# Hybrid mixer and expert block on one core: weight loads of one tile (1 MB) become loads of two (2 MB)

## The chip, the cores and the metric

One core of a Trainium2 chip runs the program; the seven others are idle. The metric is device time in microseconds (us). Before the change it was 1384.95 us, the median of three runs (1383.54 to 1385.8).

## What is computed

All weights are float32 and the batch is 256 tokens of width 2048. Cut to its stages, the reference is:

```
h = x + token_mixer(rmsnorm(x))          # one layer
    proj = h @ w_in                      # 2048 x 6672: q k v g | z | xs bc | dt
    retention(q, k, v) * silu(g)         # 4 heads of 256, two chunks of 128 tokens
    ssd(conv(xs, b, c), dt) * silu(z)    # 16 heads of 64, two chunks of 128 tokens
    concat(both) @ w_out                 # 2048 x 2048
h = h + hier_moe(rmsnorm(h))             # 32 experts in 4 groups; each token goes to 2
    a, u = ht @ w_gate[e], ht @ w_up[e]  # 2048 x 512 each
    out += (silu(a) * u * comb) @ w_down[e]   # 512 x 2048
out = rmsnorm(h)
```

The weights of all 32 experts are read, 384 tiles of 1 MB; those of w_in are 52 tiles and those of w_out 16.

## The kernel before, in words

A weight tile is 128 partitions by 2048 floats: 8 KB a partition, 1 MB, one DMA on SP's queue. The host (`lay_out`) stores each so that a partition's 8 KB stand together.

The program has three stages. **The mixer** takes w_in in 13 chunks of 512 columns, four tiles each (`win_tiles`, `first_tiles` for the first chunk). `load` puts a tile into the pool `ring`, which holds four, and `split` makes of each 128x512 part a rounded copy `wh` (ACT, L285) and a remainder `wl` (DVE, L150) in six stage buffers; TensorE (PE) multiplies both (`form_a` L367 to L369, `form_b` L355 to L357). Convolution, scan, retention and gates are generators that `pump` advances between the products; the tokens' inverse norm is one of them (`rms1`: psr, L264; rm on DVE; rcol on POOL; dg on DVE; psb, L271; rbc). **The output projection** (`out_rows`) does the same with w_out.

**The experts** come in eight groups of four, `NG = 8`. A group takes 16 gate tiles, 16 up tiles and 16 down tiles (`project` and `finish`, matmuls at L950); `gather` brings the tokens' rows, at most 32 an expert, into `xg`, and `back` adds the results (psc, L981). In the last four down tiles of a group each holds 128 output columns, so each is followed by its own `back`. The tiles go into 22 buffers, in an order written out by hand as a string of pool names: pools a (4), b (6), e (6), n (1), o (2) and three of four 8 KB "quarters" (c, d, f), which held the mixer's inputs; the fourth quarter is `xg`:

```
    cycle = "aaaaeeeeeecdfbbbbbb"
    turns = "eeeeeenbbbbb" + "baaaaeeeeeencdfbbbbb" + "o" * ONCE
```

A buffer is loaded again once the matmuls that read it are done. n and o are given up after the first group's up product, so 19 buffers go round. Every DMA signals one of eight semaphores in turn, and SP waits before it issues one for the DMA eight issues ago. A scheduler places the instructions of each engine; the program's text gives the order of the loads.

Of the kernel before, what the change touches and what calls it, by code (L numbers as in the profile page):

```python
# [18 lines left out]
P = 128  # L19
D = 2048  # L20
# [75 lines left out]
def lay_out(inp):  # L96
# [8 lines left out]
    win = np.empty((len(CHUNKS), 4, P, 4, 512), np.float32)  # L105
# [6 lines left out]
    o["wout"] = c(np.stack([wo[ET_ORDER[n], :, n].reshape(4, 4, P, 512).transpose(0, 2, 1, 3) for n in range(4)]))  # L112
    wr = np.concatenate([a["w_router_group"][0], a["w_router_expert"][0]], axis=1)
    o["wr"] = c(wr.reshape(KT, P, 36).transpose(1, 0, 2))
    for n, k in (("gate", "w_expert_gate"), ("up", "w_expert_up")):
        o[n] = c(a[k][0].reshape(NG, GE, KT, P, F).transpose(0, 2, 3, 1, 4))
    wd = a["w_expert_down"][0].reshape(NG, GE, 4, P, 4, 512)
    dn = np.empty((NG, 4, 4, P, GE, 512), np.float32)
    dn[:, :3] = wd[..., :3, :].transpose(0, 4, 2, 3, 1, 5)
    dn[:, 3] = wd[..., 3, :].reshape(NG, GE, 4, P, 4, 128).transpose(0, 4, 3, 1, 2, 5).reshape(NG, 4, P, GE, 512)  # L120
    o["down"] = dn
# [21 lines left out]
def block_kernel(tc, I, out):  # L143
# [36 lines left out]
    qp = sb("quarters")  # L180
# [15 lines left out]
    def quarter(i, n, dt=F32):  # L196
        return qp.tile([P, n, 2048 // n], dt, tag=f"q{i}", name=f"quarter{i}")
# [15 lines left out]
    # the tensor engine's clock rises while the first loads are under way  # L213
# [6 lines left out]
    # ---- normalised input (transposed, its norm weight applied), split into two float32r parts  # L220
    xraw = hp.tile([P, KT, T], F32, tag="h", name="xraw")
    xhs = [quarter(0, 8, F32R), xq.tile([P, 8, T], F32R, name="xh2")]
    xls = [quarter(1, 8, F32R), xq.tile([P, 8, T], F32R, name="xl2")]
# [23 lines left out]
    def squares():  # L247
        # summed over the tiles on the engine that is free
        a, b = quarter(2, 8)[:, :4], quarter(3, 8)[:, :4]
# [50 lines left out]
    def pump(n):  # L300
        # a step of the work that waits: what frees the accumulators first, then the mixers
# [17 lines left out]
    def first_tiles():  # L319
        sp.dma_start(par, I["par"])  # L320
        w = ring.tile([P, 4, 512], F32, tag="w", name="w")
        for a, b in ((0, 1), (1, 2), (2, 4)):
            load_x(a, b)
            sp.dma_start(w[:, a:b], I["win"][0, 0, :, a:b])
        for a, b in ((0, 1), (1, 2), (2, 4)):
            prep_x(a, b)
            for j, wh, wl in split(w[:, a:b], min(SPLIT, b - a)):
                yield a + j, wh, wl
        for i in range(1, 4):
            w = ring.tile([P, 4, 512], F32, tag="w", name="w")  # L330
            for a in (0, 2):
                load_x(4 * i + a, 4 * i + a + 2)
                sp.dma_start(w[:, a:a + 2], I["win"][0, i, :, a:a + 2])
            if i == 3:
                sp.dma_start(con, I["con"])
            for a in (0, 2):
                prep_x(4 * i + a, 4 * i + a + 2)
                for j, wh, wl in split(w[:, a:a + 2], SPLIT):
                    yield 4 * i + a + j, wh, wl

    def win_tiles(ci):
# [3 lines left out]
        for i in range(4):  # L345
            for j, wh, wl in split(load(I["win"][ci, i]), SPLIT):
                yield 4 * i + j, wh, wl
# [26 lines left out]
    # ---- state space mixer: convolution  # L374
# [59 lines left out]
    def step_sizes(xdt):  # L434
        # dt: softplus as max(v, 0) + 2 atanh(e / (2 + e)), e = exp(-|v|)
# [19 lines left out]
        # cumulative sums of dt * a: a row per head and chunk, to be spread over the partitions, and columns  # L455
# [18 lines left out]
    # rotary tables  # L474
# [28 lines left out]
    def scan(xdt):  # L503
        # state space mixer: the two chunks
# [43 lines left out]
    # ---- retention  # L548
# [20 lines left out]
    def retention(qT, kT):  # L569
        # scores[s, l] of a chunk's queries with the keys of its own chunk and of the one before  # L570
# [44 lines left out]
    # ---- gates, norms and the transposed mixer output, split in two  # L615
# [37 lines left out]
    for ci, (n, half) in enumerate(CHUNKS):  # L653
# [26 lines left out]
        elif n == "bc":  # L680
            qT, kT = (quarter(i, 8).rearrange("p (h a) t -> p h a t", h=RH) for i in (2, 3))
# [4 lines left out]
        elif n == "z":  # L686
            if half == 0:
                finish_all(later)
                ys = [quarter(i, 8, F32R).rearrange("p (a k) t -> p a k t", a=2) for i in (2, 3)]
            soon.append(group_norm(half))  # L690
            soon.append(to_yt(xs[:, :, 512 * half:512 * half + 512], 8 + 4 * half, ys[half][:, 0], ys[half][:, 1]))
    yrh, yrl = quarter(0, 8, F32R), quarter(1, 8, F32R)
# [3 lines left out]
    # ---- output projection  # L696
    def acc_pair(pool, tag):
        return [pool.tile([P, 512], F32, tag=tag, name="po") for _ in range(NT)]

    def out_rows(ps, n, ld, i0, i1, ahead=0):  # L700
        # the first tokens' products with the last rows may come ahead of the others'
        late = []
        for i in range(i0, i1):
            for j, wh, wl in split(ld(I["wout"][n, i]), SPLIT):
# [22 lines left out]
    # the first columns take the state space mixer's rows first, while the other rows are made  # L727
# [6 lines left out]
    # ---- residual and router logits; from here one ring takes the weights  # L734
# [5 lines left out]
    cycle = "aaaaeeeeeecdfbbbbbb"  # L740
    turns = "eeeeeenbbbbb" + "baaaaeeeeeencdfbbbbb" + "o" * ONCE
    turns += cycle * ((12 + NG * 48 - 32 - len(turns)) // len(cycle))
    turns = itertools.chain(turns, itertools.cycle("aaaaeeeeeebbbbbb"))

    def slot(n, name="wt"):
        if n in "cdf":
            return quarter("cdf".index(n), 4)
        return rings[n].tile([P, 4, 512], F32, tag="w", name=name)

    def wload(src):  # L750
        w = slot(next(turns))
        sp.dma_start(w, src)
        return w

# [12 lines left out]
    def residual(n):  # L767
        # logits as rows of experts, from two tiles of h at a time in two halves of the array
# [15 lines left out]
    def mean_squares():  # L784
        # of all but the last columns
# [12 lines left out]
    def residual_last(t):  # L798
# [8 lines left out]
        # (the squares themselves go where the transposes were, and aren't read)  # L807
# [6 lines left out]
    # ---- routing: first maximum of the groups, first two maxima of the group's experts  # L814
# [3 lines left out]
    # (the groups' logits are padded to eight columns)  # L818
# [10 lines left out]
    # values to be marked, behind others that don't occur: the largest of the groups, the two largest experts  # L829
# [40 lines left out]
    # the other columns: the retention's rows of all, then the state space mixer's rows of each  # L870
# [15 lines left out]
    def choose(t):  # L886
        # positions in the experts' lists, from 1; 0 where the expert isn't chosen
# [22 lines left out]
    rings["o"] = sb("wonce", bufs=ONCE, reuse_waits="tile")  # L910
# [4 lines left out]
    # ---- experts: groups of four, CAP slots each  # L915
# [22 lines left out]
    def gather(pos, cmb):  # L938
# [3 lines left out]
        xg = quarter(3, KT)  # L942
# [198 lines left out]
```

## Time and profile before

| what | value |
|---|---|
| time, median of three runs | 1384.95 us |
| span of the profiled execution | 1382.1 us (the profile gives no other time of this execution) |
| PE busy | 1109.8 us, 80% |
| DVE, ACT, POOL busy | 416.2, 271.4, 25.0 us |
| read from HBM | 481.65 MB, 350 GB/s over the span |
| SP's queue | 70610 packets, 483.80 MB |

The span runs from the first to the last instruction. A packet is what one DMA engine moves in one piece; the 16 DMA engines work beside each other. "Share" of DMA is the packets' time over the time of 16 engines, and it can pass 100% where packets of an engine overlap. Landing is the time from a DMA's issue to its last byte's signal. MB are millions of bytes in totals; a 1 MB tile is 1,048,576 bytes.

### The profile page before, as it was taken

The numbers are of one execution on the slowest core, as the hardware profiler recorded it, in microseconds if no ns is written. First come the engines' busy times: TensorE is split into PE (matmuls) and PEld (weight loads), VectorE is DVE, ScalarE is ACT, GpSimd is POOL, SyncE is SP. The second block draws the span as 40 slices with busy tenths as digits, with TensorE's granted clock in tenths as the row PEclk, the third lists the DMA queues.
The fourth block names the chain that finished last, engine by engine and source line by source line (L and its number), as shares of the span: only waits on it lengthen the run. The fifth ranks groups of instructions, "written<-read, shape, count | busy, mean of one in ns | idle before, by whom it ended". The sixth has DMA issues, their size and how long they took to land.

```text
span 1382.1 us, 17740 instructions
## 1 busy us (share of the span) xinstructions
PE 1109.8 (80%) x7323; PEld 586.3 (42%) x7323; DVE 416.2 (30%) x842; ACT 271.4 (20%) x504; POOL 25.0 (2%) x29
## 2 busy tenths in 40 slices
PE   7999999999999986686668668666866866686764
PEld 4989999888787441032014103201310320140112
DVE  8577968666555130021002002100200210020013
ACT  5465544465444000000000000000000000000002
POOL 5000000000000000000000000000000000000000
PEclk8999999999999998689669768967976886696677
DMA  7545555585876999999999999999999999999994
GB/s 270 210 159 186 198 186 196 204 324 204 337 279 212 386 419 419 420 419 419 420 420 420 419 420 420 419 420 420 420 420 420 419 419 420 420 419 420 420 419 193
DMA packets 70695, 484.98 MB, mean 351 GB/s; under 512 B 8113, under 2 KB 8785, under 8 KB 13137
## 3 DMA queue, kind: packets, MB, share of 16 engines
q1 hardware_dynamic: 70610, 483.80, 86.8%
q8 instruction: 59, 0.97, 0.3%
q14 instruction: 26, 0.21, 0.0%
HBM read 481.65 MB, written 2.11 MB: 350 GB/s over the span
## 4 chain that ended last, share of the span: by engine, by line
DMA 62%; PE 35%; DVE 1%; issue 1%; ACT 0%; SPq 0%; POOL 0%; POOLq 0%; ACTq 0%; DVEq 0%
DMA wt<-down 19%; DMA wt<-up 17%; DMA wt<-gate 16%; DMA quarter<-gate 4%; PE pb L355 4%; PE pb L357 4%; PE pb L356 4%; PE pf L368 3%; PE pf L369 3%; PE pf L367 3%; DMA quarter<-up 3%; PE po L716 2%; PE po L714 2%; PE po L715 2%; DMA quarter<-down 1%; PE pxg L924 1%
## 5 line engine op out<-in xcount | busy, mean ns | idle before, releaser
L950 PE MATMUL pu<-wt,quarter 128*32 128x512 f32 x904 | 171.8, 856 | 80.0 <-DMA wt<-up 80.0
L950 PE MATMUL pg<-wt,quarter 128*32 128x512 f32 x832 | 154.8, 832 | 76.8 <-DMA wt<-gate 76.8
L150 DVE TENSOR_TENSOR wl<-w,wh 128x512 fp32r<-128x512 f32 x224 | 158.9, 720 | 72.0 <-ACT wh L285 71.0
L150 DVE TENSOR_TENSOR sg<-sg,pu 128x512 f32<-128x512 f32 x8 | 5.5, 688 | 553.0 <-PE pu L950 551.8
L285 ACT ACTIVATE wh<-w 128x512 fp32r<-128x512 f32 x224 | 140.1, 631 | 150.5 <-PE pb L356 74.0
L950 PE MATMUL py<-wt,at 128*32 128x128 f32 (+1 forms) x1672 | 120.1, 406 | 13.7 <-DMA wt<-down 12.9
L950 PEld LDWEIGHTS pu<-wt,quarter 128*32 128x32 f32 x904 | 24.2, 127 | 223.8 <-DMA wt<-up 209.7
L950 PEld LDWEIGHTS pg<-wt,quarter 128*32 128x32 f32 x832 | 19.5, 123 | 201.3 <-DMA wt<-gate 195.6
L981 PE MATMUL psc<-y,swt 128*128 128x128 f32 (+1 forms) x224 | 75.0, 459 | 32.8 <-ACT y L978 32.8
L150 DVE TENSOR_TENSOR acc<-acc,psc 128x128 f32<-128x128 f32 (+1 forms) x98 | 43.2, 459 | 164.8 <-PE psc L981 164.6
L950 PEld LDWEIGHTS py<-wt,at 128*32 128x32 f32 x1672 | 45.3, 110 | 79.7 <-issue 39.1
L935 ACT ACTIVATE swt<-psw 128x256 f32<-128x256 f32 x8 | 3.1, 383 | 335.0 <-PE psw L933 335.0
L978 ACT ACTIVATE y<-py 128x128 f32<-128x128 f32 (+1 forms) x56 | 23.2, 414 | 225.9 <-PE py L950 225.8
L924 PEld LDWEIGHTS pxg<-selr,h 128*128 128x128 f32 x512 | 64.3, 208 | 6.5 <-issue 5.9
L924 PE MATMUL pxg<-selr,h 128*128 128x128 f32 x512 | 66.0, 292 | 0.6 <-ACT mask L1012 0.6
L981 PEld LDWEIGHTS psc<-y,swt 128*128 128x128 f32 x224 | 34.0, 194 | 76.1 <-ACT y L978 63.2
L355 PE MATMUL pb<-xh,wh 128*128 128x256 f32 x224 | 64.2, 286 | 0.0
L355 PE MATMUL pb<-quarter,wh 128*128 128x256 f32 x224 | 63.8, 285 | 0.0
L357 PE MATMUL pb<-quarter,wl 128*128 128x256 f32 x224 | 63.7, 284 | 0.0
L967 ACT ACTIVATE sg<-pg 128x512 f32<-128x512 f32 x8 | 4.8, 597 | 299.5 <-PE pg L950 299.5
L356 PE MATMUL pb<-quarter,wh 128*128 128x256 f32 x224 | 63.4, 283 | 0.0
L357 PE MATMUL pb<-xh,wl 128*128 128x256 f32 x224 | 62.8, 280 | 0.0
(259 smaller groups left out, 1466.2 us busy)
## 6 DMA issues: line engine op xcount, KB each, us to landing
wt<-up SPq DMA_DIRECT2D x113, 1024.0 KB, 19.9
wt<-down SPq DMA_DIRECT2D x113, 1024.0 KB, 19.9
wt<-gate SPq DMA_DIRECT2D x104, 1024.0 KB, 19.9
w<-win SPq DMA_DIRECT2D x48, 1024.0 KB, 4.9
quarter<-gate SPq DMA_DIRECT2D x24, 1024.0 KB, 19.9
quarter<-down SPq DMA_DIRECT2D x15, 1024.0 KB, 19.9
quarter<-up SPq DMA_DIRECT2D x15, 1024.0 KB, 19.9
wt<-wout SPq DMA_DIRECT2D x12, 1024.0 KB, 7.8
```

The lines of the kernel that those rows point to most:

```text
L150: dve.tensor_tensor(o, a, b, op=op)
L285: act.activation(wh, w[:, i:i + n], AF.Copy)
L355: pe.matmul(o, wh[:, s], xh(k), start=(k == 0 and c % 2 == 0), stop=False, skip_group_check=True)
L356: pe.matmul(o, wh[:, s], xl(k), start=False, stop=False, skip_group_check=True)
L357: pe.matmul(o, wl[:, s], xh(k), start=False, stop=(k == KT - 1), skip_group_check=True)
L367: pe.matmul(ps[t], lh(k)[:, s], wh, start=(k == 0), stop=False)
L368: pe.matmul(ps[t], lh(k)[:, s], wl, start=False, stop=False)
L369: pe.matmul(ps[t], ll(k)[:, s], wh, start=False, stop=(k == KT - 1))
L714: pe.matmul(ps[t], yh[:, s], wh, start=(k == 0), stop=False)
L924: pe.matmul(px[:, i], h[:, t, (k0 + i) * P:(k0 + i + 1) * P], selr[:, t], start=(i == 0 and x == 0), stop=(x == NT - 1), skip_group_check= ...
L950: pe.matmul(ps[s], lhsT[:, s], w(j), **k)
L981: pe.matmul(px, swt[:, t * P:(t + 1) * P], y, start=True, stop=True)
```

## The change

Weights are laid out and loaded in pairs of tiles, 16 KB a partition, 2 MB a DMA, in the order in which they are used. The rings hold pairs: `ring` (a) two, b three, e three, n one, o one; the four quarters become two "twins" of 16 KB (c and d), and `xg` gets a pool of its own. That is ten pairs that go round and twelve before the first is used again. The 8 KB for `xg` and the rest come from a smaller DMA scratch (`SCRATCH = 256`). The w_out tiles are paired over column chunks, by `OUT_ORDER`. The last two pairs of the last group are still loaded as four 1 MB halves. The final norm's rows lie in c and d.

```
-RING_A = 4
-RINGS = {"a": RING_A, "b": 6, "e": 6, "n": 1}
-ONCE = 2
+RING_A = 2
+RINGS = {"a": RING_A, "b": 3, "e": 3, "n": 1}
+SCRATCH = 256
+OUT_ORDER = [(0, i) for i in range(4)] + [(n, i) for n in range(1, 4) for i in range(2)]
+OUT_ORDER += [(n, i) for i in (2, 3) for n in range(1, 4)]
...
-        win[i] = w[:, s:s + 512].reshape(4, 4, P, 512).transpose(0, 2, 1, 3)
+        win[i] = w[:, s:s + 512].reshape(2, 8, P, 512).transpose(0, 2, 1, 3)
...
+    o["wexp"] = c(ex.reshape(NG, 24, 2, P, GE, 512).transpose(0, 1, 3, 2, 4, 5).reshape(NG, 24, P, 2 * GE, 512))
...
-    def quarter(i, n, dt=F32):
-        return qp.tile([P, n, 2048 // n], dt, tag=f"q{i}", name=f"quarter{i}")
+    def twin(i, n, dt=F32):
+        return qp.tile([P, 2, n, 2048 // n], dt, tag=f"h{i}", name=f"twin{i}")
...
     def load(src):
-        w = ring.tile([P, 4, 512], F32, tag="w", name="w")
+        w = ring.tile([P, 8, 512], F32, tag="w", name="w")
         sp.dma_start(w, src)
...
+        for i, parts in enumerate((((0, 1), (1, 2), (2, 4), (4, 6), (6, 8)), ((0, 2), (2, 4), (4, 6), (6, 8)))):
+            w = ring.tile([P, 8, 512], F32, tag="w", name="w")
...
-    cycle = "aaaaeeeeeecdfbbbbbb"
-    turns = "eeeeeenbbbbb" + "baaaaeeeeeencdfbbbbb" + "o" * ONCE
-    turns += cycle * ((12 + NG * 48 - 32 - len(turns)) // len(cycle))
-    turns = itertools.chain(turns, itertools.cycle("aaaaeeeeeebbbbbb"))
+    cycle = "aaeeecbbbd"
+    turns = "eeebbb" + "naaeeecbbbdo"
+    turns += cycle * ((6 + NG * 24 - 16 - len(turns)) // len(cycle))
+    turns = itertools.chain(turns, itertools.cycle("aaeeebbb"))
...
+    def stream(src, n, single=0):
+        for i in range(n // 2):
+            w = slot(next(turns))
+            s = src(i)
+            for p in ((0, 4), (4, 8)) if i >= n // 2 - single else ((0, 8),):
+                sp.dma_start(w[:, slice(*p)], s[:, slice(*p)])
+            yield w[:, :4]
+            yield w[:, 4:]
...
-        xg = quarter(3, KT)
+        xg = xgp.tile([P, KT, P], F32, name="xg")
...
+    def group(g):
+        return stream(lambda i: I["wexp"][g, i], 48, 2 if g == NG - 1 else 0)
...
-    nc = bacc.Bacc("TRN2", target_bir_lowering=False, num_devices=1)
+    nc = bacc.Bacc("TRN2", target_bir_lowering=False, num_devices=1, dynamic_dma_scratch_size=SCRATCH)
```

The scheduler places some instructions anew. On PE, in the fourth of the second chunk's 128-row parts (pb is that chunk's sum), the first product of the tokens' norm (psr) stood before like this, and psb nine rows on:

```order
L357 MATMUL pb<-quarter_115,wl 128x256
L355 MATMUL pb<-quarter_115,wh 128x256
L356 MATMUL pb<-quarter_117,wh 128x256
L357 MATMUL pb<-quarter_115,wl 128x256
L264 MATMUL psr<-ones,sq 128x1 x2
L355 MATMUL pb<-quarter_115,wh 128x256
L356 MATMUL pb<-quarter_117,wh 128x256
```

Here PE had products of the chunk to do before and after psr. In the changed program psr and psb stand at the end of the first chunk (pf):

```order
L371 MATMUL pf<-wh,xl_120 128x512
L274 MATMUL psr<-ones,sq 128x1 x2
L281 MATMUL psb<-dg,ones 128x256
L357 MATMUL pb<-twin_118,wh 128x256
L358 MATMUL pb<-twin_118,wh 128x256
L357 MATMUL pb<-twin_118,wh 128x256
L358 MATMUL pb<-twin_118,wh 128x256
L359 MATMUL pb<-twin_118,wl 128x256
```

They are now side by side, with none of the chunk's products between them, and four products with wh alone come before the first with wl. DVE's part of the norm (rm, dg, rbc) stood before behind ten splits, of which the last eight are the second chunk's:

```order
L150 TENSOR_TENSOR wl<-w,wh 128x512 x10
L150 TENSOR_TENSOR wdt<-wdt,par 128x256
L159 TENSOR_SCALAR rm_450<-psr 128x2
L157 TENSOR_SCALAR dg<-con,rcol 128x128 x2
L272 COPY rbc<-psb 128x256
L150 TENSOR_TENSOR wl<-w,wh 128x512 x13
```

In the changed program it stands here:

```order
L157 TENSOR_TENSOR wl<-w,wh 128x512 x2
L166 TENSOR_SCALAR rm_449<-psr 128x2
L164 TENSOR_SCALAR dg<-con,rcol 128x128 x2
L282 COPY rbc<-psb 128x256
L157 TENSOR_TENSOR wl<-w,wh 128x512 x8
```

The two splits ahead are the first chunk's last, so all of the second chunk's splits now come behind rbc. The order of the loads on SP is otherwise as before, with one row of a pair for two of a tile.

## Rows read from the trace of the kernel before

**Rows 1.** The page, busy tenths of 40 slices of 34.55 us, the whole span.
```profile
PE   7999999999999986686668668666866866686764
...
DMA  7545555585876999999999999999999999999994
GB/s 270 210 159 186 198 186 196 204 324 204 337 279 212 386 419 419 420 419 419 420 420 420 419 420 420 419 420 420 420 420 420 419 419 420 420 419 420 420 419 193
```
**Rows 2.** The page, the chain that ended last: shares of the span.
```profile
DMA 62%; PE 35%; DVE 1%; issue 1%; ACT 0%; SPq 0%; POOL 0%; POOLq 0%; ACTq 0%; DVEq 0%
```
**Rows 3.** All waits of PE's queue from 50 to 446 us: total, times, longest.
```profile
PE pht L805 <- DVE h L150: 0.5, 1, 0.5
PE psb L271 <- DVE dg L157: 0.5, 1, 0.5
```
**Rows 4.** The chain in order of time, experts: start us, us, what.
```profile
529.16 19.87 DMA wt<-gate
549.10 19.89 DMA wt<-up
...
1352.86 1.11 PE py L950 x8
```
**Rows 5.** DMA queue from 490 to 1350 us: packets, MB, share of 16 engines.
```profile
DMA packets 49513, 360.89 MB, mean 420 GB/s; under 512 B 5495, under 2 KB 5495, under 8 KB 5495
...
q1 hardware_dynamic: 49472, 360.28, 101.0%
```
**Rows 6.** DMA queue from 241 to 244 us, the load of h alone.
```profile
q1 hardware_dynamic: 79, 1.29, 100.5%
```
**Rows 7.** DMA queue from 110.6 to 111.4 us, one 1 MB tile alone.
```profile
q1 hardware_dynamic: 40, 0.33, 97.5%
```
**Rows 8.** SP's issues around the first use of the experts: start, us, operation.
```profile
420.32 24.64 SPq L752 DMA_DIRECT2D wt<-up  x5
450.52 0.33 SPq L752 DMA_DIRECT2D wt<-down  x1
```
**Rows 9.** PE's timeline, first group's gate product: the third and fourth tile.
```profile
452.56 1.92 PE L950 MATMUL pg<-wt,quarter 128*32 128x512 f32 x16
```
**Rows 10.** PE's timeline around the tokens' norm: start, us, operation [idle before].
```profile
42.28 0.28 PE L355 MATMUL pb<-quarter,wh 128*128 128x256 f32 x1
42.40 0.28 PE L356 MATMUL pb<-quarter,wh 128*128 128x256 f32 x1
...
48.04 0.50 PE L264 MATMUL psr<-ones,sq 128*128 128x1 f32 x4
...
50.10 0.70 PE L271 MATMUL psb<-dg,ones 128*128 128x256 f32 x2 [0.51 <-DVE dg L157]
50.45 0.47 PE L357 MATMUL pb<-quarter,wl 128*128 128x256 f32 x1
```
**Rows 11.** DVE's timeline there: the first splits behind rbc.
```profile
51.38 2.61 DVE L150 TENSOR_TENSOR wl<-w,wh 128x512 fp32r<-128x512 f32 x4
```
**Rows 12.** PE's timeline, the end of the last group.
```profile
1348.27 1.92 PE L950 MATMUL py<-wt,at 128*32 128x512 f32 x16
...
1352.86 1.06 PE L950 MATMUL py<-wt,at 128*32 128x512 f32 x8 [1.43 <-DMA wt<-down]
1354.64 3.52 PE L981 MATMUL psc<-y,swt 128*128 128x512 f32 x4 [0.72 <-ACT y L978]
```
**Rows 13.** ACT's timeline: two splits in a row of the second chunk.
```profile
36.88 0.63 ACT L285 ACTIVATE wh<-w 128x512 fp32r<-128x512 f32 x1 [0.77 <-PE pf L369]
38.28 0.63 ACT L285 ACTIVATE wh<-w 128x512 fp32r<-128x512 f32 x1 [0.77 <-PE pf L369]
```
**Rows 14.** DMA issues by line: count, KB each, median us to landing.
```profile
w<-win SPq DMA_DIRECT2D x48, 1024.0 KB, 4.9
...
h<-x SPq DMA_DIRECT2D x1, 2048.0 KB, 8.0
```

More of the change, by code (lines that the diff above doesn't have):

```diff
@@ L179, in block_kernel @@
     hp = sb("h")
-    qp = sb("quarters")
+    qp = sb("halves")
+    xgp = sb("gathered")
     sta, stb = (sb("stage" + n, bufs=STAGE // 2) for n in "ab")
@@ L247, in squares @@
     def squares():
[L249 removed]
+        ab = twin(1, 8)
+        a, b = ab[:, 0, :4], ab[:, 1, :4]
         for i in range(4):
@@ L320, in first_tiles @@
         sp.dma_start(par, I["par"])
[L321 to L334, printed above, removed]
+        for i, parts in enumerate((((0, 1), (1, 2), (2, 4), (4, 6), (6, 8)), ((0, 2), (2, 4), (4, 6), (6, 8)))):
+            w = ring.tile([P, 8, 512], F32, tag="w", name="w")
+            for a, b in parts:
+                load_x(8 * i + a, 8 * i + b)
+                sp.dma_start(w[:, a:b], I["win"][0, i, :, a:b])
+            if i == 1:
                 sp.dma_start(con, I["con"])
[L336 to L339, printed above, removed]
+            for a, b in parts:
+                prep_x(8 * i + a, 8 * i + b)
+                for j, wh, wl in split(w[:, a:b], SPLIT):
+                    yield 8 * i + a + j, wh, wl
     def win_tiles(ci):
@@ L344, in win_tiles @@
             return
-        for i in range(4):
+        for i in range(2):
             for j, wh, wl in split(load(I["win"][ci, i]), SPLIT):
-                yield 4 * i + j, wh, wl
+                yield 8 * i + j, wh, wl
     def form_b(ci):
@@ L680, in block_kernel @@
         elif n == "bc":
-            qT, kT = (quarter(i, 8).rearrange("p (h a) t -> p h a t", h=RH) for i in (2, 3))
+            qkT = twin(1, 8)
+            qT, kT = (qkT[:, i].rearrange("p (h a) t -> p h a t", h=RH) for i in range(2))
             later.append(scan(xdt))
@@ L703, in out_rows @@
         for i in range(i0, i1):
-            for j, wh, wl in split(ld(I["wout"][n, i]), SPLIT):
+            for j, wh, wl in split(out_quarter(OUT_ORDER.index((n, i)), ld), SPLIT):
                 k = 4 * i + j
@@ L909, in block_kernel @@
     ep = sb("experts", reuse_waits="tile")
-    rings["o"] = sb("wonce", bufs=ONCE, reuse_waits="tile")
+    rings["o"] = sb("wonce", reuse_waits="tile")
     for p in (pm, pa):
@@ L957, in pbank, with finish @@
         return pg.tile([P, 512], F32, tag=name, name=name, bufs=bufs)
-    def finish(xg, swt, pgate, usrc, dsrc, after_up=None, done=None, first=False):
+    def finish(xg, swt, pgate, ws, after_up=None, done=None, first=False):
         if done:
@@ L962, in finish @@
         pup = pbank("pu")
-        project(pup, xg, ((k, wload(usrc(k))) for k in range(KT)))
+        project(pup, xg, ((k, next(ws)) for k in range(KT)))
         if ew is None:
@@ L988, in finish @@
             for f in range(4):
-                w = wload(dsrc(n, f))
+                w = next(ws)
                 cols(py, at[:, f], lambda j: w[:, j], start=(f == 0), stop=(f == 3))
@@ L992, in finish @@
         for n in range(4):
-            w = wload(dsrc(3, n)).rearrange("p e (f n) -> p e f n", f=4)
+            w = next(ws).rearrange("p e (f n) -> p e f n", f=4)
             py = pbank("py", 2)
@@ L998, in finish @@
         return nxt
-    xg = quarter(3, KT)
+    def group(g):
+        return stream(lambda i: I["wexp"][g, i], 48, 2 if g == NG - 1 else 0)
+    xg = xgp.tile([P, KT, P], F32, name="xg")
     pgate = pbank("pg")
+    ws = group(0)
     for k0, n in ((0, 1), (1, 1), *((k, 2) for k in range(2, KT, 2))):
         gather_part(xg, k0, n, (0, 1) if n == 1 else (1, 0))
-        project(pgate, xg, ((k, wload(I["gate"][0, k])) for k in range(k0, k0 + n)))
+        project(pgate, xg, ((k, next(ws)) for k in range(k0, k0 + n)))
     room = mask.rearrange("p t e -> p (t e)").bitcast(F32)
@@ L1042, in final_tiles @@
     def final_tiles():
-        for n, r in (("w", "c"), (0, "d"), (1, "f")):
-            fin[n] = slot(r, "fin").rearrange("p a b -> p (a b)")
-        row = slot("a", "row").rearrange("p a b -> p (a b)")[:1]
+        s, r = ((x.rearrange("p a b -> p (a b)")) for x in (slot("c"), slot("d")))
+        fin["w"], fin[0], fin[1], row = s[:, :D], s[:, D:], r[:, :D], r[:1, D:]
         one = ep.tile([1, P], F32, name="one")
@@ L1089, in block_kernel @@
             pgate = pbank("pg")
-            project(pgate, xg, ((k, wload(I["gate"][g, k])) for k in range(KT)))
+            ws = group(g)
+            project(pgate, xg, ((k, next(ws)) for k in range(KT)))
         if g + 1 < NG:
             e = slice(GE * g + GE, GE * g + 2 * GE)
-            xg, swt = finish(xg, swt, pgate, lambda k: I["up"][g, k], lambda n, f: I["down"][g, n, f],
-                             lambda: gather(posm[:, :, e], comb[:, :, e]), first=(g == 0))
+            xg, swt = finish(xg, swt, pgate, ws, lambda: gather(posm[:, :, e], comb[:, :, e]), first=(g == 0))
         else:
-            finish(xg, swt, pgate, lambda k: I["up"][g, k], lambda n, f: I["down"][g, n, f], None, final_part)
+            finish(xg, swt, pgate, ws, None, final_part)
     final_norm()
@@ L1105, in block_kernel @@
             gd = bass.ds(gi, 1)
-            def at_g(name, *i):
-                return I[name][(gd, *i)].rearrange("a p e f -> p (a e) f")
+            ws = stream(lambda i: I["wexp"][gd, i].rearrange("a p e f -> p (a e) f"), 48)
             xg, swt = gather(posm[:, :, :GE], comb[:, :, :GE])
             pgate = pbank("pg")
-            project(pgate, xg, ((k, wload(at_g("gate", k))) for k in range(KT)))
-            finish(xg, swt, pgate, lambda k: at_g("up", k), lambda n, f: at_g("down", n, f))
+            project(pgate, xg, ((k, next(ws)) for k in range(KT)))
+            finish(xg, swt, pgate, ws)
             for a in (posm, comb):
```

39 lines of the change are left out of this document (25 added, 14 removed).

## The prediction

> **What bounds the kernel now.** I read the slices first [rows 1]. They show two stages. Up to slice 13 (some 450 us) PE is busy nearly all the time and the DMA engines are not; from slice 14 to the last but one the DMA engines are full, at 419 or 420 GB/s, and PE has time to spare. The chain of waits says the same in shares: DMA 62%, PE 35% [rows 2]. So there are two places in which the change can move the end. In the first, every stall of PE counts: from 50 to 446 us PE waited twice in all, 0.5 us each time [rows 3]. In the second, what counts is how fast a tile comes in, how many are in when the flow starts, and what is left to do after the last ones.
>
> The flow can be read from the chain [rows 4]. Each of its DMA pieces lasts 19.9 us, and the next starts 19.94 us after the one before (529.16 to 549.10). SP waits for the DMA of eight issues ago, so eight tiles lie between: 19.94 / 8 = 2.49 us a tile, 4.985 us for two. The chain leaves the DMA at 1352.86 us, when the tile (column chunk 2, rows 3) of the last group is in; 29.2 us of work follow.
>
> **The rate, the largest term.** A tile is 128 packets of 8 KB, eight for each of the 16 engines, so an engine needs 2.49 / 8 = 311.6 ns a packet. From the queue's row for 490 to 1350 us, leaving out the 5495 small packets that signal completion, 43,977 packets took 101.0% of 16 x 860 us: 316.0 ns each [rows 5]. That is more than 311.6 because packets of one engine overlap a little.
>
> What would a 16 KB packet take? The trace has them: h is loaded in rows of 16 KB, and while that load was alone 79 packets moved 1.29 MB, so they are whole 16 KB packets, and took 1.005 x 16 x 3.0 us / 79 = 610.6 ns each [rows 6]. A tile alone shows 0.975 x 16 x 0.8 us / 40 = 312 ns for 8 KB [rows 7]. So, alone, 16 KB in one piece take 13 ns less than in two. What eight transfers in the queue add is 316.0 - 312 = 4 ns for an 8 KB packet. I have three values for a 16 KB packet in a full queue, against 2 x 311.6 = 623.1 ns now:
> - nothing is added: 610.6 ns, 2.0% less;
> - 4 ns once a packet: 614.6 ns, 1.4% less;
> - 4 ns for each 8 KB: 618.6 ns, 0.7% less.
>
> I take the middle one: 8 x 614.6 = 4.917 us for a pair, 0.068 us less than now. The outer ends are no gain (4.985), should the bytes alone set the pace in a full queue, and 3.4% (316.0 x 2 against 610.6), should the overlap come on top.
>
> How many pairs does this count for? The pairs pass through the flow from the first reuse of a buffer to the tile at 1352.86: 190 of the 192 pairs, less the 12 that are loaded before: 178. 178 x 0.068 = **12.1 us** saved (6.4 and 17.8 at the inner ends, 0 and 30 at the outer).
>
> The Trainium skill, "DMA: Bandwidth & Descriptors", section "Where 436 GB/s comes from", puts the ceiling of a core's 16 ports at 435.2 GB/s; by it, as an estimate, a pair could not take less than 4.819 us, and the term could not pass 30 us. The 420 GB/s of [rows 1] lie 3.5% under that ceiling, so the trace agrees that there is room, and how much of it a longer packet takes only the 610.6 ns tell.
>
> **The start of the flow.** Before, 22 tiles found a free buffer ahead of the first reuse; the last of these was issued at about 445 us, and reuse began at 450.52, when the first gate tile had been used [rows 8]. Now 24 tiles have a place, two more (4.985 us of flow). But the first buffer to come round (a) holds gate tiles 2 and 3, which are done at 452.56 + 1.92 = 454.48 us [rows 9], 3.96 us later. Net **-1.0 us**. This needs the 24 to be in by then. The last of them, o, waits for the routing's last products, as its tiles did before (445 us, the end of the first piece of [rows 8]); at 5 us a pair it lands in time.
>
> **The norm's products.** Before, psr and psb cost PE 0.50, a wait of 0.51, and 0.35 up to the next product: 1.4 us [rows 10]. Now they stand where the second chunk begins (42.28 us before), and DVE makes none of that chunk's remainders until rbc is done. From psr to DVE's first split behind rbc is 51.38 - 48.04 = 3.34 us, and one split lasts 2.61 / 4 = 0.65 [rows 10, 11]: the first product that needs wl comes 4.0 us after psr. Ahead of it PE has four products of the chunk, 0.12 us apart [rows 10], 0.5 us. So PE loses 3.5 us where it lost 1.4: **+2.1 us**. PE has no idle time before 446 us in which this could be made up [rows 3], so it delays the flow's start. Its bounds are 0 (if DVE's lead had been used up anyway) and 3.5.
>
> **The end.** Chunk 2's last two row tiles of the last group now land together. Two tiles take PE 1.92 us in one go, one takes 1.06 [rows 12]: **+0.9 us** after the same landing. Behind it PE, not the DMA, sets the pace (psc alone is 3.52 us while 1 MB lands every 2.49), so the four last halves of 1 MB are in before they are used.
>
> **Edits that I cost at nothing.** In the mixer a pair is asked for when DVE has split the last part of the pair before the previous one, eight parts before it is needed. Parts follow each other by 1.40 us (36.88 to 38.28) [rows 13], so there are 11.2 us. The one 2 MB load of the trace landed in 8.0 us and a 1 MB load in 4.9 [rows 14]; that leaves 3 us, and behind them the splits that are ahead of PE. If this cover were gone, PE would stall once a pair: see the second rival. Fewer issues on SP save nothing, since SP waits for landings. Ten pairs that go round are 20 tiles where there were 19; with eight pairs in flight the DMA engines would run dry only in a pause of PE of 8 x 4.9 = 39 us, longer than all the work behind the last landing in the chain (29.2 us). xg's own pool, the padding of c and d and the final norm's rows move no work.
>
> **The sum.** -12.1 - 1.0 + 2.1 + 0.9 = -10.1 us, against the profiled execution's span of 1382.1: 1372.0. That execution has no other time than its span; the median of the runs, 1384.95, lies 2.85 us above it, which I add: **1374.9 us**. Without any gain in rate it would be 1384.95 + 2.0 = 1387.0.
>
> **The rivals.**
> *The bytes set the pace, and the packet's length gains little.* In a full queue an engine then needs between 618.6 and 623.1 ns for 16 KB, saves 0 to 6.4 us, and the time is 1380.6 to 1387.0. For it speaks that 312 and 610.6 ns come from windows of one load each; against it, that the 13 ns are in both. The case that rows are cut into 8 KB packets all the same belongs here, and the packets of h speak against it. A rule on a packet's fixed part bears on this: the Trainium skill, same page, section "Why small descriptors are slow (HBM only)", gives a packet a fixed 3 cycles beside its bytes in 32-byte beats. By that, as an estimate, a 16 KB packet saves 3 of 518 cycles, 0.6%, about 5 us of flow, and the time is about 1382. The 13 ns of [rows 6, 7] are more than that rule's 3 or 4 ns, so the trace does not bear it out alone. Chance of the rival: 17%.
>
> *The mixer starves* (the other side). SP is one queue: a pair's load stands behind the scan's 256 KB loads, each of which waits for PE, and one late issue now costs eight parts instead of four. The place is the first 360 us, 24 pairs. The point from which it decides is a landing later than the 11.2 us of cover plus the splits ahead; every us beyond that is paid by PE. Half a us a pair gives back the 12.1 us; 1 us a pair makes 1374.9 + 24 = 1399. For it speaks that 3 us of margin rest on one load; against it, that PE did not wait once with a margin of the same kind before [rows 3]. Chance: 9%.
>
> *The overlap comes on top.* 3.4% of 887 us are 30 us: 1387.0 - 30 = 1357. The end would then also be nearer to PE's own pace. Chance: 5%.
>
> **How the numbers follow.** The forecast (a gain of 6.4 to 17.8 us in rate: 1369 to 1381) has the other 69%. A measurement of this kernel can tell about 0.2%, 2.8 us, from no change: faster means under 1382.2, slower over 1387.7. The forecast and the third rival are faster, and a fourth of the first rival: 0.78. Most of the rest of the first rival is within: 0.12. The second rival and the first's upper edge with a larger loss at the norm are slower: 0.10. The range from 1366 to 1385 holds the forecast with up to 3 us for the small terms, and two thirds of the first rival.
>
> **What would show it.** In the profile after: GB/s in the full slices at 426 rather than 420; half the packets; pieces of the chain 39.3 us long (eight pairs); 16 KB packets of 613 to 620 ns by the queue's row; psb with a wait of some 1.5 us at 44 us, and the next product with wl some 1 us behind it; SP's first reuse near 456.6 us; the last chain piece ending near 1342 and 30 us after it. Wrong would be: 420 GB/s as before (first rival), or rows of PE waiting for splits or loads between 50 and 440 us (second).

## The result and the profile after

The changed kernel took **1370.11 us**, median of four runs (1368.65 to 1375.7), beside 1385.38 us for the kernel before on the same chip: a ratio of 0.990 (95% interval 0.987 to 0.992), 15 us less. A second set gave 1371.28 us and 0.990 (0.988 to 0.991). The profiled execution took 1369.11 us, its span is 1367.3 us, 14.8 us under the span before.

The page of the changed kernel, the traffic in 40 slices of 34.2 us, to be held against [rows 1], and the chain's shares:

```profile
GB/s 264 177 151 189 192 193 202 195 323 193 327 301 223 365 426 427 427 427 427 428 427 426 426 429 426 425 427 428 428 425 427 426 427 428 427 427 426 428 425 222
...
DMA 63%; PE 34%; DVE 1%; issue 1%; ACT 0%; SPq 0%; POOL 0%; POOLq 0%; DVEq 0%; ACTq 0%
```

The full slices moved 419 or 420 GB/s and now move 425 to 429; the chain's shares are those of [rows 2]. The chain in order of time (start us, us, what), to be held against [rows 4]:

```profile
521.21 39.14 DMA twin<-wexp
560.40 39.14 DMA wt<-wexp
599.61 40.49 DMA twin<-wexp
...
1309.94 33.45 DMA wt<-wexp
...
1343.53 0.81 PE py L973 x18
```

From 521.21 to 560.40 are 39.19 us for eight pairs, 4.90 us a pair; before it was 4.985. Of the 19 whole pieces between 521 and 1272 us four are some 1.2 us longer, as four were 1.5 us longer before. The queue's rows for 490 to 1340 us:

```profile
DMA packets 25017, 362.74 MB, mean 427 GB/s; under 512 B 2770, under 2 KB 2770, under 8 KB 2770
...
q1 hardware_dynamic: 24978, 362.15, 100.3%
```

That is half the packets of [rows 5]: 22,208 of 16 KB.

**Where the 14.8 us came from.** Three stretches add up to the span: to SP's first reuse of a buffer (450.52 before [rows 8]), from there to the start of chunk 2's last row tiles in the last group (1352.86 before [rows 4]), and the rest.

| stretch | before, us | after, us | difference | foretold |
| --- | --- | --- | --- | --- |
| up to the first reuse | 450.52 | 458.13 | +7.6 | +6.1 (3.96 by the buffer's place, 2.1 by the norm) |
| the flow | 902.34 | 882.83 | -19.5 | -17.1 (12.1 of rate, 4.985 of two more tiles) |
| behind it | 29.24 | 26.34 | -2.9 | +0.9 |
| span | 1382.1 | 1367.3 | -14.8 | -10.1 |

The rows of the changed kernel for these borders, SP's timeline and PE's (start us, us, operation [idle before and what ended it]):

```profile
458.13 0.33 SPq L774 DMA_DIRECT2D wt<-wexp  x1
```
```profile
452.98 1.92 PE L973 MATMUL pg<-wt,xg 128*32 128x512 f32 x16
...
1340.96 1.92 PE L973 MATMUL py<-wt,at 128*32 128x512 f32 x16 [2.90 <-DMA wt<-wexp]
1343.53 0.81 PE L973 MATMUL py<-wt,at 128*32 128x128 f32 x18 [0.65 <-DMA wt<-wexp]
1344.28 1.98 PE L1004 MATMUL psc<-y,swt 128*128 128x512 f32 x4
```

The x16 are two row tiles that landed together; before, the last one came alone [rows 12].

### The profile page after: what moved, and what is told of

Read it like the earlier page. It is cut to its first block, busy times and chain, and to the rows that moved or that the text cites. A ratio compares the mean times of both kernels' runs of the same rounds, so it can differ in the third digit from the quotient of the medians.

```text
span 1367.3 us, 17274 instructions
## 1 busy us (share of the span) xinstructions
PE 1051.8 (77%) x7323; PEld 597.3 (44%) x7323; DVE 415.9 (30%) x842; ACT 271.4 (20%) x504; POOL 25.6 (2%) x29
## 4 chain that ended last, share of the span: by engine, by line
DMA 63%; PE 34%; DVE 1%; issue 1%; ACT 0%; SPq 0%; POOL 0%; POOLq 0%; DVEq 0%; ACTq 0%
DMA wt<-wexp 39%; DMA twin<-wexp 23%; PE pb L357 4%; PE pb L359 4%; PE pb L358 4%; PE pf L370 3%; PE pf L371 3%; PE pf L369 3%; PE po L729 2%; PE po L727 2%; PE po L728 2%; PE pg L973 1%; PE pu L973 1%; PE pxg L947 1%; DMA w<-win 1%
## 5 line engine op out<-in xcount | busy, mean ns | idle before, releaser
L973 PE MATMUL pu<-wt,xg 128*32 128x512 f32 x864 | 144.3, 798 | 95.9 <-DMA wt<-wexp 95.9
L973 PE MATMUL pg<-wt,xg 128*32 128x512 f32 x832 | 135.7, 782 | 84.3 <-DMA wt<-wexp 84.2
L973 PE MATMUL py<-wt,at 128*32 128x128 f32 (+1 forms) x1456 | 112.7, 418 | 19.0 <-DMA wt<-wexp 19.0
L973 PEld LDWEIGHTS pu<-wt,xg 128*32 128x32 f32 x864 | 28.8, 129 | 208.5 <-DMA wt<-wexp 157.3
L973 PEld LDWEIGHTS pg<-wt,xg 128*32 128x32 f32 x832 | 25.8, 127 | 182.5 <-DMA wt<-wexp 136.2
L1004 PE MATMUL psc<-y,swt 128*128 128x128 f32 (+1 forms) x224 | 70.8, 439 | 25.9 <-ACT y L1001 25.1
L357 PE MATMUL pb<-twin,wh 128*128 128x256 f32 x224 | 64.4, 288 | 0.6 <-ACT wh L295 0.6
L359 PE MATMUL pb<-twin,wl 128*128 128x256 f32 x224 | 64.2, 288 | 0.0
L358 PE MATMUL pb<-twin,wh 128*128 128x256 f32 x224 | 64.0, 286 | 0.0
L947 PEld LDWEIGHTS pxg<-selr,h 128*128 128x128 f32 x512 | 60.0, 196 | 6.5 <-issue 5.9
L358 PE MATMUL pb<-xl,wh 128*128 128x256 f32 x224 | 62.7, 280 | 0.0
```

Of the source, the lines that this page charges most:

```text
L357: pe.matmul(o, wh[:, s], xh(k), start=(k == 0 and c % 2 == 0), stop=False, skip_group_check=True)
L358: pe.matmul(o, wh[:, s], xl(k), start=False, stop=False, skip_group_check=True)
L359: pe.matmul(o, wl[:, s], xh(k), start=False, stop=(k == KT - 1), skip_group_check=True)
L947: pe.matmul(px[:, i], h[:, t, (k0 + i) * P:(k0 + i + 1) * P], selr[:, t], start=(i == 0 and x == 0), stop=(x == NT - 1), skip_group_check= ...
L973: pe.matmul(ps[s], lhsT[:, s], w(j), **k)
L1004: pe.matmul(px, swt[:, t * P:(t + 1) * P], y, start=True, stop=True)
```

## The experiments

**What a packet costs by its length.** A kernel of loads alone; here its loads in short, not in the words of the program.

```
48 x  sp.dma_start(w[:, 2048-wide part], v[x])              # 1 MB, 8 KB rows
24 x  sp.dma_start(w[:, 4096-wide part], v[x])              # 2 MB, 16 KB rows
24 x  sp.dma_start(w[:, 4096-wide part] as p a r, v[x])     # 2 MB, 8 KB rows
48 x  sp.dma_start(w[q:q + 64, 4096-wide part], v[x, q:q + 64])
12 x  sp.dma_start(w, v[x])                                 # 4 MB, 32 KB rows
48 x  sp.dma_start(w[:, 2048-wide part] as p a r, v[x])     # 1 MB, 4 KB rows
24 x  sp.dma_start(w[:, 4096-wide part], v[x])              # 2 MB, 16 KB rows
```

> This kernel leaves the whole computation out: it only loads 48 MB of weights in each of seven ways, one after the other on SP's queue, nothing else running. Theory (a packet has a fixed part of some 11 ns beside its bytes, whatever the DMA's size): 1 MB DMAs with 8 KB rows 311.6 ns a packet, 2.49 us a MB; 2 MB with 16 KB rows 612.5 ns, 4.90 us for 2 MB; 2 MB with 8 KB rows as the first, 4.985 us for 2 MB; 1 MB with 16 KB rows on 64 partitions as the second, 4.90 us for 2 MB; 4 MB with 32 KB rows 1214 ns, 9.72 us; 4 KB rows 161 ns, 2.58 us a MB. Rival A (what costs is the DMA, its semaphore and its issue, not the packet): 2 MB with 8 KB rows 4.90 us, 1 MB with 16 KB rows 4.985 us, 4 KB rows 2.49 us. Rival B (rows on half of the partitions are slower for another reason): the fourth way is slower than both 4.90 and 4.985.

The queue's rows inside the first six ways, from 40:100, 150:210, 270:330, 400:560, 600:680 and 745:805 us:

```profile
DMA packets 3479, 25.31 MB, mean 422 GB/s; under 512 B 389, under 2 KB 389, under 8 KB 389
...
DMA packets 1765, 25.72 MB, mean 429 GB/s; under 512 B 195, under 2 KB 195, under 8 KB 195
...
DMA packets 3282, 25.31 MB, mean 422 GB/s; under 512 B 192, under 2 KB 192, under 8 KB 192
...
DMA packets 2629, 34.42 MB, mean 215 GB/s; under 512 B 528, under 2 KB 528, under 8 KB 528
...
DMA packets 1181, 34.51 MB, mean 431 GB/s; under 512 B 128, under 2 KB 128, under 8 KB 128
...
DMA packets 6375, 24.59 MB, mean 410 GB/s; under 512 B 373, under 2 KB 373, under 8 KB 6375
```

Sixteen engines times the window, over the packets less the small ones (16 x 60 us / 3090 for the first): 310.7 ns for 8 KB in 1 MB loads, 611.5 for 16 KB, 310.7 for 8 KB in 2 MB loads, 1218 for 16 KB on 64 partitions, 1216 for 32 KB, 160.0 for 4 KB. (32 KB packets come in bursts; the window 640:700 gives 1202. The seventh way repeats the second and moved 429 GB/s again.) The size of the DMA changes nothing, the packet's length does: 8 and 16 KB give 10 ns a packet and 301 ns for each 8 KB; 4 KB (160.4 by that) and 32 KB (1213) fit. The theory held but for the fourth way, where rival B was right; rival A fell. A longer packet is also a longer row in HBM here, so whether the 10 ns lie with the engine or with the start of a row is not shown.

**The same in the kernel: 2 MB loads in 8 KB packets.**

```
-    o["wexp"] = c(ex.reshape(NG, 24, 2, P, GE, 512).transpose(0, 1, 3, 2, 4, 5).reshape(NG, 24, P, 2 * GE, 512))
+    o["wexp"] = c(ex.reshape(NG, 24, 2, P, GE, 512))
...
-            for p in ((0, 4), (4, 8)) if i >= n // 2 - single else ((0, 8),):
-                sp.dma_start(w[:, slice(*p)], s[:, slice(*p)])
+            for p in ((0, 1), (1, 2)) if i >= n // 2 - single else ((0, 2),):
+                sp.dma_start(w.rearrange("p (a e) f -> p a e f", a=2)[:, slice(*p)], s[:, slice(*p)])
...
-        return stream(lambda i: I["wexp"][g, i], 48, 2 if g == NG - 1 else 0)
+        return stream(lambda i: I["wexp"][g, i].rearrange("a p e f -> p a e f"), 48, 2 if g == NG - 1 else 0)
```

> The changed kernel with its 2 MB loads of the experts kept, but each made of two rows of 8 KB per partition, 256 packets of 8 KB instead of 128 of 16 KB. Theory (the packet's length is what the rate came from): a pair again takes 4.985 us, DMA pieces of the chain 39.9 us, 178 x 0.085 = 15 us slower than the changed kernel: about 1385. Rival A (fewer DMAs, semaphores and issues gave it): pieces of 39.14 us and about 1370, no difference.

1385.46 us, a ratio to the kernel before of 1.000 (0.999 to 1.001): the whole gain is gone. The chain's pieces:

```profile
539.25 32.86 DMA wt<-wexp
574.11 32.87 DMA wt<-wexp
```

They are shorter than expected, since a load of 256 packets was issued only some 33 us ahead of its landing: 34.86 us from one to the next hold seven pairs, not eight. That is 4.98 us a pair, and the traffic is 420 GB/s again (490 to 1340 us). So the gain in rate came from the packets' length.

**16 KB packets in 1 MB loads.** Each pair in two loads of 64 partitions.

```
-            for p in ((0, 4), (4, 8)) if i >= n // 2 - single else ((0, 8),):
-                sp.dma_start(w[:, slice(*p)], s[:, slice(*p)])
+            for p, q in ((P, (0, 4)), (P, (4, 8))) if i >= n // 2 - single else ((64, (0, 8)),):
+                for r in range(0, P, p):
+                    sp.dma_start(w[r:r + p, slice(*q)], s[r:r + p, slice(*q)])
```

> The changed kernel with each pair of the experts loaded by two DMAs of 1 MB, the first with the 16 KB rows of partitions 0 to 63, the second with those of 64 to 127: as many DMAs and as many bytes in flight as before the change, but packets of 16 KB. Theory (the packet's length): 4.90 us a pair, about 1370, DMA pieces of 19.6 us. Rival A (the number of DMAs): 4.985 us a pair, about 1385. Rival B (64 partitions at a time are slower in themselves): more than 1390.

2034.81 us (1887.58 to 2133.01): a miss for the theory as a forecast, and no test of it, since these loads on half of the partitions ran at half the rate, here from 600 to 900 us:

```profile
DMA packets 4984, 65.28 MB, mean 218 GB/s; under 512 B 999, under 2 KB 999, under 8 KB 999
```

The Trainium skill, "SBUF — State Buffer", section "Door 1: The DMA port swizzle", says that partitions 0 to 63 reach only 8 of the 16 ports, some 218 GB/s; the 215 GB/s of the load kernel and the 218 of this row agree. Later in this execution the traffic rose, up to 376 GB/s in one slice of 52 us; why is not shown.

**The norm's products put back.**

```
-    def load(src):
+    def load(src, halves=False):
         w = ring.tile([P, 8, 512], F32, tag="w", name="w")
-        sp.dma_start(w, src)
+        for p in ((0, 4), (4, 8)) if halves else ((0, 8),):
+            sp.dma_start(w[:, slice(*p)], src[:, slice(*p)])
...
-            for j, wh, wl in split(load(I["win"][ci, i]), SPLIT):
+            for j, wh, wl in split(load(I["win"][ci, i], ci == 1), SPLIT):
```

> The changed kernel with the second chunk's first pair loaded as two halves of 1 MB, by which the scheduler puts the norm's products psr and psb back behind the fourth part of the second chunk, where they stood before the change. Theory (the changed kernel lost 3.6 us there: some 2.1 in the wait for dg, rbc and the first remainder, and 1.5 because PE's clock fell after that wait): psb waits about 0.5 us, no low clock between 46 and 50 us, the first group's gate products 3.6 us earlier (452.6 instead of 456.2), the whole about 3.6 us faster: ratio to the changed kernel 0.9974, about 1366.5. Rival (only the 2.1 us come back, the clock falls later all the same): 454 us and 1368. Rival (the DMA sets the flow's start, not PE): the gate products come earlier, the end stays at 1370.

1368.74 us, ratio to before 0.988 (0.986 to 0.990). PE's timeline at the norm, first the changed kernel, where before is in [rows 10]:

```profile
42.24 0.50 PE L274 MATMUL psr<-ones,sq 128*128 128x1 f32 x4
44.30 0.70 PE L281 MATMUL psb<-dg,ones 128*128 128x256 f32 x2 [1.56 <-DVE dg L164]
45.60 0.38 PE L357 MATMUL pb<-twin,wh 128*128 128x256 f32 x1 [0.60 <-ACT wh L295]
...
46.33 0.52 PE L359 MATMUL pb<-twin,wl 128*128 128x256 f32 x1
```

Then this experiment:

```profile
49.03 0.50 PE L274 MATMUL psr<-ones,sq 128*128 128x1 f32 x4
51.10 0.70 PE L281 MATMUL psb<-dg,ones 128*128 128x256 f32 x2 [0.51 <-DVE dg L164]
...
450.45 1.93 PE L974 MATMUL pg<-wt,xg 128*32 128x512 f32 x16
```

And the stretches of 4 us there (us; PE busy, granted clock, DMA share, GB/s), the changed kernel and the experiment:

```profile
42.00:46.00 4.00, 1.84 (x11) 1.00 0.61 262
46.00:50.00 4.00, 4.00 (x21) 0.57 0.02 4
50.00:54.00 4.00, 4.00 (x36) 1.00 0.41 78
```
```profile
42.00:46.00 4.00, 4.00 (x30) 1.00 0.62 262
46.00:50.00 4.00, 4.00 (x36) 1.00 0.43 84
50.00:54.00 4.00, 3.49 (x27) 1.00 0.94 401
```

In the changed kernel PE stood for 2.2 us in two waits, and in the 4 us behind them its clock was granted at 0.57, near the lower of its two levels (1.2 of 2.4 GHz): products came every 0.21 us instead of every 0.12, as in these two rows of the changed kernel:

```profile
48.14 0.41 PE L357 MATMUL pb<-twin,wh 128*128 128x256 f32 x1
48.35 0.41 PE L358 MATMUL pb<-twin,wh 128*128 128x256 f32 x1
```

With the products put back the low clock isn't seen, and of the waits only the 0.51 for dg that stood there before the change. In the experiment the second chunk began at 43.28 us, 1.0 us later than in the changed kernel (42.24), for another reason; from there to the first gate product it took 407.2 us, the changed kernel 410.7, the kernel before 407.1. So the norm's place cost 3.6 us. The other runs agree: from the second chunk's start to the first warm-up product (pidle) it took 402.8 to 404.3 us in seven executions with the norm early, 399.9 in three with it put back and in the kernel before, and 401.0 in a fourth with it put back where PE also waited 1.1 us for the scan. The time alone, 1368.74, lies between the theory's 1366.5 and the 1370 of no gain, and does not decide: of the 2.5 us by which the first gate product came earlier, 1.0 was lost again at the end, where the last row tiles ran at a granted clock of 0.60 instead of 1.00.

**A buffer that comes round earlier.**

```
-    turns = "eeebbb" + "naaeeecbbbdo"
+    turns = "eeebbb" + "aaeeecbbbdno"
```

> The changed kernel with the pool n taken ahead of o instead of first, so that pool a holds gate tiles 0 and 1 and is the first buffer to come round. Theory (the flow starts when the first buffer comes round and DMA has nothing to do before, a gap of 3 us near 458 us in the changed kernel): first reuse 3.1 us earlier, near 454.9 us, no gap near 458 us, the whole 3 us faster: about 1367, ratio to the changed kernel 0.998. Rival (the 24 tiles are still coming in then, so an earlier reuse only waits in the queue): 1370.

1368.48 us, ratio 0.987 (0.985 to 0.989). In its profile (SP's timeline, then PE's):

```profile
458.12 0.33 SPq L774 DMA_DIRECT2D wt<-wexp  x1
```
```profile
449.28 4.20 PE L925 MATMUL pidle<-onb,lowb 128*128 128x128 bf16 x43
...
456.14 1.92 PE L973 MATMUL pg<-wt,xg 128*32 128x512 f32 x16
```

The reuse came 1.98 us behind the first gate product instead of 5.15, the 3.2 us expected, but that product itself was 3.2 us later: psr stood 2.2 us later in this execution, of which 1.5 were left at the first warm-up product, and the warm-up products (pidle) took 1.6 us more, at a granted clock of 0.59 instead of 1.00. The absolute 454.9 us was a miss for that reason, and the times alone would not settle a gain of this size.

**One pair fewer ahead of the first reuse.**

```
-    turns = "eeebbb" + "naaeeecbbbdo"
+    turns = "eeebbb" + "naaeeecbbbd"
```

> The changed kernel without the pool o: 22 tiles instead of 24 have a place ahead of the first reuse, as before the change. Theory (each pair that is in before the first reuse saves the flow one pair): 4.9 us slower than the changed kernel, about 1375, DMA idle some 8 us ahead of 458 us instead of 3. Rival (the two tiles were not in by then anyway): 1370.

1376.76 us, ratio 0.994 (0.992 to 0.996). From the first reuse (462.92) to chunk 2's last row tiles (1350.70) it took 887.8 us, 4.95 more than with o: one pair. DMA moved nothing from 454 to 461 us.

**Chunk 2's tiles landing singly.**

```
-        return stream(lambda i: I["wexp"][g, i], 48, 2 if g == NG - 1 else 0)
+        return stream(lambda i: I["wexp"][g, i], 48, 4 if g == NG - 1 else 0)
```

> The changed kernel with the last four pairs of the last group loaded as halves, not only the last two. Theory (two tiles of chunk 2 that land together cost 0.9 us at the end): 0.7 us faster, 1369.4, which the time alone can hardly show; in the profile the last row tile of chunk 2 starts 2.5 us behind the one before it and takes 1.06 us. Rival (PE's chain behind chunk 2 sets the end, whatever lands when): no difference, the same length from the last landing that PE waits for to the end, some 24 us.

1370.96 us, ratio 0.990 (0.988 to 0.991): no difference that the time shows. The last row tile of chunk 2:

```profile
1345.94 1.07 PE L973 MATMUL py<-wt,at 128*32 128x512 f32 x8 [1.19 <-DMA wt<-wexp]
1347.73 1.98 PE L1004 MATMUL psc<-y,swt 128*128 128x512 f32 x4 [0.72 <-ACT y L1001]
```

From its start to the end are 25.4 us, 1.0 less than the 26.3 from the x16 above, of which 0.1 lie behind the last norm. So the 0.9 us were there, as small as foretold.

**The mixer's loads in halves.** Every w_in and w_out load as two of 1 MB, on top of the edit that puts the norm back.

```
-            for j, wh, wl in split(load(I["win"][ci, i], ci == 1), SPLIT):
+            for j, wh, wl in split(load(I["win"][ci, i], True), SPLIT):
...
-            outw = ld(I["wout"][u // 2])
+            outw = ld(I["wout"][u // 2], True)
```

> The changed kernel with every load of the mixer and of the output projection made as two halves of 1 MB with 8 KB rows, so only the experts keep 2 MB loads; the norm's products then also stand behind the fourth part of the second chunk. Theory (the mixer's loads are hidden in either form): no wait of PE between 50 and 440 us, the same time as the run that only moves the norm, about 1368.7. Rival (pairs delay the mixer's loads, or the longer packets help it): more than 2 us to either side of that.

Inconclusive as a time: 1369.33, 1369.52, 1376.12 and 1376.17 us. In its profile PE waits for no load and no split from 50 to 443 us, only once 1.1 us for a scan's de and 0.5 for dg, and the flow has its 882.8 us.

**Both gains together**, the norm's place and the order of n: the edits above, joined, beside the changed kernel once more and a step further, where pools b and e hold one buffer of four tiles (B, E) and one of two each. The main lines of that step's edit:

```
-RINGS = {"a": RING_A, "b": 3, "e": 3, "n": 1}
+RINGS = {"B": 16, "b": 8, "E": 16, "e": 8, "n": 8}
...
-    turns = "eeebbb" + "naaeeecbbbdo"
...
+    cycle = ["aa", "E", "ec", "B", "bd"]
+    turns = itertools.chain(cycle, ["no"], cycle * ((NG * 12 - 8 - 6) // 5), itertools.cycle(["aa", "E", "eb", "B"]))
...
-                sp.dma_start(w[:, slice(*p)], s[:, slice(*p)])
...
+                    sp.dma_start(w[:, p:q], s[:, at + p:at + q])
```

> The changed kernel unaltered, beside the next two on the same chip. Theory (the norm's place lowers PE's clock behind it): psb waits 1.56 us again and the granted clock is below 1 in the 4 us behind it; 1370, within 0.2%. Open: whether the 48 warm-up products ahead of the experts' first gather take 2.6 us, as in the profile of the changed kernel, or 4.2 to 4.5, as in four experiments that kept the norm's place.

> The changed kernel with two edits of the earlier experiments together: the norm's products behind the fourth part (first pair of the second chunk in halves), and the pool n ahead of o. Theory (the two gains add up, as both move the flow's start, one by PE and one by the buffer): psr near 48 to 49 us, first gate product near 450.5, first reuse near 452.4, then 882.7 us to the last row tiles of chunk 2 and 26.4 to the end: a span near 1361.5 and a time of 1363.5, ratio to before 0.984. Rival (d and o are still coming in at 452.4, so the earlier reuse waits in the queue): the flow is longer by what it waits, at most 3 us, and the time 1366.

> As the run with both edits, and of every five groups of four tiles two are loaded by one DMA of 4 MB with rows of 32 KB (pools b and e as one buffer of four tiles and one of two); the last 4 MB of the last group as four loads of 1 MB, the 4 MB ahead as two. Theory (a packet has a fixed part; the load kernel showed 1205 ns for 32 KB against 2 x 611.5): four tiles in 32 KB rows 9.64 to 9.70 us instead of 9.80, over 2/5 of 89 groups of four 4 to 6 us less: a time near 1358.5. Rival (four tiles that land together and are freed together make PE wait and the DMA run dry): 1363.5 or more, and pauses of the DMA beyond the four of 1.2 us.

Both together: **1364.58 us** (1363.89 to 1365.71), ratio to before 0.985 (0.984 to 0.986), beside 1371.28 for the changed kernel, where each edit alone had a ratio of 0.988 and 0.987. SP's timeline, then PE's:

```profile
452.62 0.33 SPq L775 DMA_DIRECT2D wt<-wexp  x1
```
```profile
450.63 1.92 PE L974 MATMUL pg<-wt,xg 128*32 128x512 f32 x16
...
1335.89 1.92 PE L974 MATMUL py<-wt,at 128*32 128x512 f32 x16 [1.95 <-DMA wt<-wexp]
```

The flow took 883.3 us from 452.62 and the span is 1362.1, where 882.7 and 1361.5 were foretold: the gains add up, 0.6 us short in the flow; the time is 1.1 us over its forecast. The changed kernel again: psb waited 1.56 us, the clock behind it was granted at 0.57, the warm-up products took 4.20 us and the first reuse came at 460.85, 8.2 us later than with both edits, 1.6 of it by the warm-up products.

The groups of four: 1365.44 us, ratio 0.985 (0.984 to 0.987), no gain over both that the time shows. Its traffic rose by 1 GB/s only:

```profile
DMA packets 19756, 359.50 MB, mean 428 GB/s; under 512 B 2191, under 2 KB 2191, under 8 KB 2191
```

From the first reuse (455.30) to the end of its span (1364.7) are 909.4 us, with pairs (1362.1 - 452.62) 909.5. But the two do not spend their time in the same places. Here are chunk 2's psc in the last group (PE's timeline) and the last norm's POOL step (the chain), first in the groups of four, then in pairs:

```profile
1338.39 1.98 PE L1015 MATMUL psc<-y,swt 128*128 128x512 f32 x4 [0.71 <-ACT y L1012]
...
1350.88 0.25 POOL r L219
```
```profile
1339.21 1.98 PE L1005 MATMUL psc<-y,swt 128*128 128x512 f32 x4
...
1351.06 0.25 POOL r L219
```

From the first reuse to that psc are 883.1 us with groups of four and 886.6 with pairs (886.2 in the changed kernel): some 3 us less, of the 4 to 6 foretold. The DMA engines show the same: though the first reuse was 2.7 us later (1.6 of it by the warm-up products, 4.13 us), 6.23 MB were moved behind 1325 us, with pairs 6.58. What took the gain back lies behind the flow: from the POOL step to the end it took 13.8 us instead of 11.0, a stretch that took 13.3 before the change and 13.0 in the run with the mixer's loads in halves. Whether the other executions lost it in the same place is not shown. That PE now waits for four tiles at once (4.95 us ahead of column chunk 1's four in the last group) goes with the rival; it was not tested apart.

## Why the prediction was right, and where its terms were off

The time, 1370.1, lay in the range, 4.8 us under the forecast, and none of the three rivals took place. By its steps:

- **The rate** was the mechanism as told, mis-sized: 0.085 us a pair instead of 0.068, 178 x 0.085 = 15.1 us instead of 12.1. The packet's own time was foretold well by "4 ns once a packet": 614.6 ns, and the queue's row gives 1.003 x 16 x 850 us / 22,208 = 614.2. The step that failed is "8 x 614.6 = 4.917 us for a pair": it sets a packet's own time, overlap included, against the pace of 2 x 311.6 ns, though the prediction itself had found that 8 KB packets last 316.0 ns at a pace of 311.6. The pace came out at 612.5 ns by the chain (4.90 us / 8), and 611.5 with loads alone. The bytes-set-the-pace rival needed over 618.6. The rule of the Trainium skill beside it (3 cycles a packet, "DMA: Bandwidth & Descriptors", "Why small descriptors are slow (HBM only)") does not agree: the fixed part of a packet measured 10 ns, more than the 3 or 4 that the prediction made of it as an estimate.
- **The start** held: the flow lost a pair (4.95 us where o was taken out), and the reuse moved by the buffer's place (3.2 us closer to the first gate product in the run with n taken later).
- **The norm** cost 3.6 us instead of 2.1. The length of the wait was sized well: the first product with wl came 4.1 us behind psr, 4.0 foretold. But the prediction saw only DVE's part of it. ACT's copies wh of the second chunk stood behind the norm as well, after a step on v that waits for rcol, so PE's first four products were late too (its second wait, 0.60, is for wh). ACT, then DVE, in the changed kernel:

```profile
43.76 1.26 ACT L563 ACTIVATE v<-pf,rcol 128x512 f32<-128x512 f32 x2 [9.09 <-POOL rcol L219]
44.92 3.23 ACT L295 ACTIVATE wh<-w 128x512 fp32r<-128x512 f32 x6
```
```profile
45.58 4.30 DVE L157 TENSOR_TENSOR wl<-w,wh 128x512 fp32r<-128x512 f32 x7
```

The first wl was done near 46.2 us and its product came at 46.33, so DVE alone would have held PE about as long; that the sum came out is in part luck. What the step "PE loses 3.5 us where it lost 1.4" left out is the clock: the next 16 products came at 0.21 or 0.22 instead of 0.12 us, some 1.5 us more.
- **The end** came out 2.9 us shorter instead of 0.9 longer. The 0.9 was there (single landings gave it back). Two things of the profiled executions lie over it: psc took 1.98 us instead of 3.52 [rows 12], with PE's clock granted at 1.00 instead of 0.55 (-1.5; why it was low before the change is not shown), and from the last norm's POOL step to the end it took 11.2 us instead of 13.3 (-2.1). The second is no part of the change: with the mixer's loads in halves it took 13.0 us. The chain's rows for that step, before and after:

```profile
1368.78 0.25 POOL r L211
```
```profile
1356.12 0.25 POOL r L219
```

- **The edits costed at nothing** cost nothing: PE waited once, 0.5 us, from 50 to 446 us, as in [rows 3].
- The misses are -3.0, +1.5 and -3.8 us, and +0.6 in the flow that no row here explains: -4.7 together, from -10.1 to -14.8. Without the -3.6 of the two things at the end the span would have missed by 1.1 us: that the norm's extra cost and the rate's extra gain offset each other in part is luck. The 2.85 us put on top of the span to come to a median were 2.8 (1370.11 - 1367.3).

## What to carry to other kernels

Where a queue is full, take a packet's price from packets of that length in a full queue, and count its fixed part by packets, not by DMAs: two rows of 8 KB in one DMA gained nothing. Keep a packet's own time and the pace apart where packets overlap. Then ask what a larger unit moves elsewhere: which buffer comes round first, and where a scheduler puts products that were hidden, on every engine; here these cost 3.2 and 3.6 us, and two small edits together won 6.7 us of time back. A wait of PE costs more than its length when the clock falls behind it, here 1.5 us more.

## What the runs showed of the hardware that was not expected

- Loads on 64 partitions moved 215 to 218 GB/s with all 16 engines shown busy (100.8% in the kernel), 1218 ns for a 16 KB packet.
- PE's granted clock fell to 0.57 in the 4 us behind two waits of 2.2 us together, while PE was busy without a gap.
- The 48 warm-up products ahead of the experts took 2.6 us in some profiles and 4.1 to 4.5 in others, in two executions of the changed kernel itself 2.58 (granted clock 1.00) and 4.20 (0.58); it is one part of why the first reuse lay between 458.1 and 463.1 us in executions alike up to there. What sets it stays open: it was seen with the norm in either place.
- A 2 MB load of 256 packets was in the queue for 33 us, one of 128 packets for 39 us, at nearly the same rate.
